# A two-layer transformer block on one core: the retention's key decay, its output scale, transposes in the first stage, earlier modulations and weights kept for the last block

## The chip, the cores and the metric

The kernel runs on one core of a Trainium2 chip. A core has TensorE (matmuls, PE in the rows; PEld is its weight load), VectorE (DVE), ScalarE (ACT), GpSimd (POOL) and SyncE (SP, which issues most DMAs). Each engine works through its own instructions in order and waits on semaphores for the others. Matmul operands lie in SBUF, results in PSUM, eight banks of 128 partitions by 512 floats. The metric is the device time of one execution in microseconds; the median of several runs is given.

## The reference

Two layers (`DEPTH` = 2) of a block on 512 tokens x and 256 context tokens z, 1024 wide:

```python
def hybrid_layer(x, z, c, c_ctx, p, rope_ret, rope_mla, need_ctx):
    mod_x = jax.nn.silu(c) @ p['w_ada'] + p['b_ada']
    mod_z = jax.nn.silu(c_ctx) @ p['w_ada'] + p['b_ada']
    ...
    hx = x * (1.0 + sc1x) + sh1x
    hz = z * (1.0 + sc1z) + sh1z
    mix_x, mix_z = token_mixers(hx, hz, p, rope_ret, rope_mla, need_ctx)
    x = layer_norm(DEEPNORM_ALPHA * x + g1x * mix_x, ...)
    x = layer_norm(DEEPNORM_ALPHA * x + g2x * sq_relu_mlp(x * (1.0 + sc2x) + sh2x, p), ...)
    (z likewise where need_ctx, that is in the first layer alone)
```

`token_mixers` sums three gated branches: retention (four heads in chunks, forward and backward, keys multiplied by a decay that depends on the position, a norm per head and a gain `ret_gn_gain`), neighbourhood attention (eight heads) and latent attention (eight heads), and multiplies the sum with `w_out`. `sq_relu_mlp` is relu squared between two weights of 1024 by 4096 and back. Six vectors of modulation per layer and token kind (shift, scale, gate, twice) come from `w_ada`.

## The kernel before

**Arithmetic.** Everything is held feature-major, 128 features in the partitions. A product in float32 accuracy is three fast matmuls: each operand is split into a high part (ScalarE, `hi_of`, line 388) and what is left (VectorE, `lo_of`, line 391), and `mm3` (lines 438 to 440) adds high by high, high by low, low by high. A weight unit is 128 by 1024 floats, 512 KB: `load` fetches it into one of three `wraw` buffers, `weight` splits it into one of three `wsp` pairs, or, with `own=True`, into two tiles of the large pool.

**Memory.** Large tiles (`dbl`, 4 KB per partition) come from a pool of 30, small ones (`sgl`, 2 KB) from one of 13. PSUM has banks of tags `pd` (three: projections and most else), `pst` (two: transposes, retention outputs), `pso` (one) and `pss` (scores).

**Order.** The Python code traces instructions; a scheduler then sets each engine's order by its own estimate of when an instruction is ready. `tc.keep_in_program_order` pins an instruction behind the one traced before it on its engine. What runs beside what is written by hand: `Fill` holds jobs (projections, gates, the retention's preparation) that are fed between the steps of a `pipeline` by their TensorE cost, and `Paced` advances a generator by a rate (`step`) or up to a count (`until`).

**Stages, in order of time.** The *opening* (lines 1592 to 1656, to about 70 us) computes conditioning, modulates the input and multiplies with the first four weights, in a loop over eight slices k of 128 features. For slice k the scale's modulation is a TensorE product (`modulation_pe`, line 495, into a `pso` bank, read at line 497); the shift's is one on VectorE (`modulation`, line 515, one product for x and one for z); `affine_split` (lines 600 to 602) forms the operands; `outer` multiplies them. Then latent attention (`mla`, to about 500 us; 40 items of three steps in the first layer, with a function `tick` called after each), neighbourhood attention (`Natten`), and retention in two runs, `ret.run(0)` and `ret.run(1)`, each prepared by `prep` as a fill job. In `prep` the rotated keys are transposed on TensorE into `pd` banks (line 1285), multiplied by the decay (line 1291, tile `ktf`), and split, tile by tile (lines 1292 and 1293). An item of the retention has scores (688, 1368), outputs (1392 to 1396), the norm (1402 to 1412) and a transposition (1419) whose result is multiplied by the gain and a half (line 1424).

The remaining modulations of the first layer (gate, shift, scale, gate: units 16 to 47) and all 48 of the second are computed on VectorE by `modulations`, one unit after another: while the gates' fill jobs run (`ADA_GATES` = 0.3 of a unit per us of fill), in the last branch (`ADA_BRANCH`), in the output product (`ADA_OUT`) and in the MLP (`ADA_MLP`). The first 24 (`ROOMY`) fetch their weights into large tiles two ahead, the rest through the single `graw` buffer. Then follow the three branches (lines 1467 to 1513), the output product with the first norm, the MLP in eight blocks j, of `ff1` (four units) and `ff2` (four units), and the second norm. In the second layer (`need` false) the first and the last block of the MLP run in two rounds of 256 tokens each, and each round loads and splits its weights anew (line 1815).

Of the kernel before, what the change touches and what calls it, by code (L numbers as in the profile page):

```python
# [10 lines left out]
BF16 = mybir.dt.bfloat16  # L11
# [6 lines left out]
D = 1024  # L18
# [17 lines left out]

WIDE = 64
# [10 lines left out]

ROOMY = 24
# [3 lines left out]
ADA_BRANCH = 0.05  # L53
# [264 lines left out]
def block_kernel(ctx, tc, xT, zT, cond, wu, sp, bias, tab, out):  # L318
# [148 lines left out]

    silu = [dram.tile([1, D], F32, name=f"silu{i}") for i in range(2)]
# [23 lines left out]
    def modulation_pe(ps, l, c, raw, v):  # L492

        for k in range(KT):
            pe.matmul(ps, raw[:, 128 * k : 128 * k + 128], v[:, :, k].unsqueeze(2).broadcast_to([128, 2, WIDE // 2]), start=k == 0, stop=k == KT - 1)
        m = mods[l][:, c, :]
        dve.tensor_scalar(m, ps[:, :, 0], 0.5, spt[l][:, SP_BADA + c : SP_BADA + c + 1], op0=ALU.mult, op1=ALU.add)
        adjust(m, c)
# [46 lines left out]
    def modulations(units, cs, roomy):  # L545

        def fetch(i):
            if i < len(units):
                t = dbl("ada") if i < roomy else graw.tile([128, 1024], F32, tag="graw", name=nm("graw"))
                sync.dma_start(t, wu[IDX[units[i][0], "ada", units[i][1]]])  # L550
                raws.append(t)

        units, raws = list(units), []
        fetch(0)
        if roomy:
            fetch(1)
        yield
        for i, u in enumerate(units):
            modulation(*u, raws[i], cs, True)
            if len(raws) < i + 2 or i + 2 < roomy:  # L560
                fetch(len(raws))
            yield
# [212 lines left out]
    def mla(l, hx, hz, need, qn, kn, kr, res, want, ahead):  # L775
# [194 lines left out]
        def tick(t):  # L970

            if t == len(items) // 2 - 4:
                fetch_values(1)
            if t == len(items) // 2 + 1:
                for _ in prep_values(1):
                    pass

# [190 lines left out]
    class Retention:  # L1168
# [39 lines left out]
        def prep(self, p2):  # L1208
# [71 lines left out]
            kt = new_tiles(512, 6)  # L1280
            for src, i0 in ((k32, 0), (kz32, 4)):
                nt = src.shape[-1] // 128
                ps = bank_d()
                for i in range(nt):
                    pe.transpose(ps[:, 128 * i : 128 * i + 128], src[:, 128 * i : 128 * i + 128], ident)
                for i in range(nt):
                    t = kt[i0 + i]
                    v = ps[:, 128 * i : 128 * i + 128].rearrange("p (h d) -> p h d", h=2).unsqueeze(2).broadcast_to([128, 2, 2, 64])
                    dk = self.kd[:, i % 2, 2 * p2 : 2 * p2 + 2, :].unsqueeze(3).broadcast_to([128, 2, 2, 64])
                    f = sgl("ktf")[:, :256]  # L1290
                    dve.tensor_tensor(f.rearrange("p (h t d) -> p h t d", h=2, t=2), v, dk, op=ALU.mult)  # L1291
                    hi_of(t[:, :256], f)
                    lo_of(t[:, 256:], f, t[:, :256])
# [53 lines left out]
        def item(self, p2, o, c):  # L1347
# [66 lines left out]
            def s2():  # L1414
# [9 lines left out]
                dve.tensor_scalar(dst, ps, spt[self.l][:, SP_GN + h : SP_GN + h + 1], 0.5, op0=ALU.mult, op1=ALU.mult)  # L1424
# [167 lines left out]
    def opening():  # L1592
# [17 lines left out]
        def inputs(k):  # L1610

            for kind in (1, 0):
                raw = dbl("ada")
                fetch_in(raw, wu[IDX[0, "ada", 8 * kind + k]])
                if kind:
                    modulation_pe(bank_o()[:, :WIDE].rearrange("p (t r) -> p t r", t=2), 0, 8 * kind + k, raw, v)
# [45 lines left out]
    for l in range(DEPTH):  # L1662
# [27 lines left out]
        mla(l, hx, hz, need, qn, kn, kr, y_mla, want[0], na.start)  # L1690
# [6 lines left out]
        if l == 0:  # L1697
            later = Paced(modulations([(0, c) for c in range(16, 48)] + [(1, c) for c in range(48)], conditioning_again(), ROOMY))
# [26 lines left out]
        for c in branch(l, 0, sizes, ops[2], g_mix, total, yop):  # L1725
            later.step(c * ADA_BRANCH)
# [20 lines left out]
        later.until(1 + 8)  # L1747
        for r, (b, cols) in enumerate(rounds):
# [25 lines left out]
            later.until(1 + 24)  # L1774
# [3 lines left out]
        acc = [new_tiles(n, KT) for _, n in bufs]  # L1778
        if need:
            hx, hz = None, None  # L1780
            h_next = [None, None]
        for j in range(8):
            apart = j in (0, 7)
            for rnd in [[r] for r in rounds] if apart else [[(b, slice(0, n)) for b, (_, n) in enumerate(bufs)]]:
# [29 lines left out]
                for i in range(4):  # L1814
                    w = weight(l, "ff2", j, i)
# [90 lines left out]
```

## Time and profile before

| | |
|---|---|
| median of 3 runs | 2592.39 us (2590.51 to 2593.95) |
| the profiled execution | 2591.01 us |
| its span, first to last instruction | 2589.2 us |
| TensorE busy | 2508.3 us (97%) |
| VectorE busy | 1749.9 us (68%) |
| ScalarE busy | 1170.0 us (45%) |
| GpSimd busy | 134.1 us (5%) |
| mean granted TensorE clock | 0.990 of full |

Matmuls are pipelined, so a busy TensorE is not one at its peak. In a line of a timeline stand the start in us, the time taken, engine, line of the kernel, operation, tiles (out<-in), shape and count, and in brackets the idle time of that engine just before and what ended it. A table of stretches gives for each its length and, by engine, the busy time in it with the number of instructions in brackets, then the granted clock (PEclk), the share of the DMA engines that were busy and GB/s.

### The profile page before, as it was taken

The page shows a single profiled execution, that of the slowest core. Times are in us where ns is not written, and L with a number is a line of the kernel's source. Part 1 is how long each engine was busy: PE and PEld are TensorE (multiplying, and loading weights), DVE is VectorE, ACT ScalarE, POOL GpSimd, SP SyncE. Part 2 cuts the span into 40 slices and gives each one's busy share as a digit, 9 for nine tenths or more (in the row PEclk, how much of TensorE's full clock was granted, in tenths as well). Part 3 has the DMA queues.
Part 4 walks back from the last instruction along what each step waited for, and adds up shares of the span by engine and source line. Part 5 has one row for each costly group of instructions (what it writes and reads, how often), then busy time and mean ns, then how long its engine had stood idle before and what let it go on. Part 6 is the DMA issues. An engine that isn't in the chain of part 4 may idle for free.

```text
span 2589.2 us, 40118 instructions
## 1 busy us (share of the span) xinstructions
PE 2508.3 (97%) x15354; PEld 2236.2 (86%) x15354; DVE 1749.9 (68%) x3432; ACT 1170.0 (45%) x2224; POOL 134.1 (5%) x121
## 2 busy tenths in 40 slices
PE   8999999999999999999999999999999899999997
PEld 7999998988888887888888888889898788988887
DVE  6566556788968885676556767665668768744457
ACT  2555545565334345222222446554556544732325
POOL 0100000111000000000000000010011000000000
PEclk8999999999999999999999999999999999999999
DMA  6322224534855533444344424323554466433333
GB/s 244 95 70 90 70 89 125 157 100 128 289 180 176 186 113 106 130 131 134 128 138 131 136 82 140 94 84 102 151 157 119 134 192 195 146 99 98 98 98 123
DMA packets 151317, 340.47 MB, mean 131 GB/s; under 512 B 18642, under 2 KB 58962, under 8 KB 151124
## 3 DMA queue, kind: packets, MB, share of 16 engines
q1 hardware_dynamic: 140756, 322.17, 40.4%
q10 hardware_dynamic: 10368, 15.73, 1.6%
q8 instruction: 121, 1.98, 0.3%
q14 instruction: 72, 0.59, 0.1%
HBM read 288.27 MB, written 36.45 MB: 125 GB/s over the span
## 4 chain that ended last, share of the span: by engine, by line
PE 80%; DVE 9%; ACT 4%; issue 4%; DMA 2%; POOL 1%; SPq 1%; POOLq 0%; ACTq 0%; DVEq 0%
PE pd L440 19%; PE pd L438 19%; PE pd L439 19%; PE pd L660 3%; PE pd L662 3%; PE pso L629 3%; PE pd L661 3%; PE pst L612 3%; DVE wsp L391 1%; PE pss L688 1%; PE pss L439 1%; PE pss L438 1%; PE pss L440 1%; PE pst L1392 1%; ACT wsp L388 1%
## 5 line engine op out<-in xcount | busy, mean ns | idle before, releaser
L438 PE MATMUL pd<-op,wsp 128*128 128x512 f32 (+1 forms) x3080 | 1069.1, 348 | 19.1 <-ACT wsp L388 5.0
L440 PE MATMUL pd<-op,wsp 128*128 128x512 f32 (+1 forms) x3080 | 1062.3, 346 | 13.7 <-DVE wsp L391 13.2
L439 PE MATMUL pd<-op,wsp 128*128 128x512 f32 (+1 forms) x3080 | 1066.5, 346 | 3.3 <-DVE op L391 1.6
L438 PEld LDWEIGHTS pd<-op,wsp 128*128 128x128 f32 x3080 | 586.0, 191 | 92.2 <-ACT wsp L388 7.0
L440 PEld LDWEIGHTS pd<-op,wsp 128*128 128x128 f32 x3080 | 585.1, 190 | 85.8 <-DVE wsp L391 15.2
L439 PEld LDWEIGHTS pd<-op,wsp 128*128 128x128 f32 x3080 | 586.7, 191 | 70.6 <-DVE op L391 3.3
L388 ACT ACTIVATE wsp<-wraw 128x1024 fp32r<-128x1024 f32 x317 | 334.1, 1055 | 390.2 <-PE pd L440 269.1
L391 DVE TENSOR_TENSOR wsp<-wraw,wsp 128x1024 fp32r<-128x1024 f32 x317 | 386.2, 1221 | 170.4 <-ACT wsp L388 169.5
L660 PE MATMUL pd<-wsp,op 128*128 128x256 f32 x704 | 202.7, 288 | 7.4 <-DVE ktf L1291 3.7
L662 PE MATMUL pd<-wsp,op 128*128 128x256 f32 x704 | 200.7, 285 | 0.5 <-DVE wsp L391 0.5
L661 PE MATMUL pd<-wsp,op 128*128 128x256 f32 x704 | 200.5, 285 | 0.0
L1793 DVE TENSOR_TENSOR rl<-rl 128x256 f32<-128x256 f32 (+1 forms) x104 | 58.9, 567 | 152.2 <-ACT rl L1792 152.1
L1792 ACT ACTIVATE rl<-pd 128x256 f32<-128x256 f32 (+1 forms) x104 | 51.9, 499 | 231.2 <-PE pd L440 230.9
L391 DVE TENSOR_TENSOR pt<-pst,pt 128x512 fp32r<-128x512 f32 (+1 forms) x208 | 121.6, 603 | 42.9 <-ACT pt L388 41.0
L660 PEld LDWEIGHTS pd<-wsp,op 128*128 128x128 f32 x704 | 136.3, 194 | 9.4 <-DVE ktf L1291 4.1
L1807 DVE TENSOR_TENSOR t<-pd,t 128x512 f32<-128x512 f32 (+1 forms) x132 | 80.9, 616 | 89.4 <-PE pd L440 89.0
L662 PEld LDWEIGHTS pd<-wsp,op 128*128 128x128 f32 x704 | 136.2, 193 | 0.7 <-DVE wsp L391 0.7
L661 PEld LDWEIGHTS pd<-wsp,op 128*128 128x128 f32 x704 | 136.3, 194 | 0.0
L388 ACT ACTIVATE pt<-pst 128x512 fp32r<-128x512 f32 (+1 forms) x208 | 105.2, 529 | 52.6 <-PE pst L612 38.3
L629 PE MATMUL pso<-pt,t 128*128 128x256 f32 x704 | 114.5, 292 | 5.1 <-DVE tx L636 2.2
L515 DVE CUSTOM_DVE_ANT_0 cond<-graw,cond,sp 128x1024 bf16<-128x1024 f32 x80 | 102.4, 1280 | 17.3 <-DMA graw<-wu 17.1
L1451 ACT ACTIVATE gate<-pd 128x512 f32<-128x512 f32 x72 | 37.8, 525 | 157.6 <-PE pd L440 153.3
(280 smaller groups left out, 3444.0 us busy)
## 6 DMA issues: line engine op xcount, KB each, us to landing
wraw<-wu SPq DMA_DIRECT2D x327, 512.0 KB, 3.7
graw<-wu SPq DMA_DIRECT2D x56, 512.0 KB, 3.6
ada<-wu SPq DMA_DIRECT2D x40, 512.0 KB, 5.6
gg<-gate ACTq DMA_DIRECT2D x48, 256.0 KB, 2.0
gl<-gg SPq DMA_DIRECT2D x48, 256.0 KB, 3.3
zbias<-bias SPq DMA_DIRECT2D x64, 128.0 KB, 2.3
t<-vd SPq DMA_DIRECT2D x28, 256.0 KB, 5.6
gd<-gt SPq DMA_DIRECT2D x40, 128.0 KB, 2.3
```

The costliest lines, as they stand in the source:

```text
L388: act.activation(R(dst), src, AF.Copy, scale=scale)
L391: (eng or dve).tensor_tensor(R(dst), src, hi, op=ALU.subtract)
L438: pe.matmul(ps, R(a[0]), R(b[0]), start=start, stop=False)
L439: pe.matmul(ps, R(a[0]), R(b[1]), start=False, stop=False)
L440: pe.matmul(ps, R(a[1]), R(b[0]), start=False, stop=stop)
L515: i = dve.tensor_tensor_reduce(cs[2], raw, cs[t], 0.5, spt[l][:, SP_BADA + c : SP_BADA + c + 1], ALU.mult, ALU.add, mods[l][:, c, t : t + 1])
L612: pe.transpose(ps[:, 128 * k : 128 * k + 128], src[:, 128 * (a + k) : 128 * (a + k) + 128], ident)
L629: pe.matmul(o, R(vts[k]), R(pts[k]), start=k == 0, stop=k == n - 1)
L660: pe.matmul(ps, R(a[0]), R(w[0][:, o : o + 256]), start=k == 0, stop=False)
L661: pe.matmul(ps, R(a[1]), R(w[0][:, o : o + 256]), start=False, stop=False)
L662: pe.matmul(ps, R(a[0]), R(w[1][:, o : o + 256]), start=False, stop=k == nk - 1)
L1807: dve.tensor_tensor(a, ps, a, op=ALU.add)
```

## The change

In `prep` all decay multiplications of a bank are issued first, into small tiles that hold two of them, and the split then takes two key tiles at a time. The scale of the retention's output moves from VectorE to ScalarE; the half is put into the gain at the start. In the opening, twelve transposes of the identity are put behind the TensorE modulation of slice 1 and six behind that of slice 2, into the same PSUM tile, ahead of the read at line 497. Units 16 to 23 of the first layer's modulations are computed in the second half of the latent attention, with large tiles of their own; the rest follow where they did, with 16 in place of 24 fetched far ahead, and none in the last branch. In the second layer's last MLP block, the `ff2` weights split in the first round are kept in large tiles for the second.

```diff
+N_STIR = {1: 12, 2: 6}
...
+ADA_EARLY = range(16, 24)
...
-ADA_BRANCH = 0.05
...
+        b = t[:, SP_GN : SP_GN + 4]
+        dve.tensor_scalar(b, b, 0.0, 0.5, op0=ALU.add, op1=ALU.mult)
...
+    def stir(ps, n):
+
+        for _ in range(n):
+            tc.keep_in_program_order(pe.transpose(ps[:, 128:256], ident, ident))
+
+    def modulation_pe(ps, l, c, raw, v, then):
 
         for k in range(KT):
             pe.matmul(ps, raw[:, 128 * k : 128 * k + 128], v[:, :, k].unsqueeze(2).broadcast_to([128, 2, WIDE // 2]), start=k == 0, stop=k == KT - 1)
+        then()
         m = mods[l][:, c, :]
...
+    def modulations_early(units):
+
+        cs = [dbl("silu") for _ in range(2)] + [dbl("prod").bitcast(BF16)[:, :D]]
+        for t in range(2):
+            sync.dma_start(cs[t], silu[t].partition_broadcast(128))
+        raws = []
+
+        def fetch(i):
+            t = dbl("ada")
+            sync.dma_start(t, wu[IDX[units[i][0], "ada", units[i][1]]])
+            raws.append(t)
+
+        fetch(0)
+        yield
+        for i, u in enumerate(units):
+            if i + 1 < len(units):
+                fetch(i + 1)
+            modulation(*u, raws[i], cs, True)
+            yield
...
+            if beside and t > len(items) // 2 + 2 and t % 2:
+                beside.advance()
+
...
-            kt = new_tiles(512, 6)
+            ktt = [dbl("kt") for _ in range(3)]
+            kt = [h for t in ktt for h in halves(t, 512)]
...
+                fs = [sgl("ktf") for _ in range(nt // 2)]
                 for i in range(nt):
-                    t = kt[i0 + i]
...
-                    f = sgl("ktf")[:, :256]
+                    f = fs[i // 2][:, 256 * (i % 2) : 256 * (i % 2) + 256]
                     dve.tensor_tensor(f.rearrange("p (h t d) -> p h t d", h=2, t=2), v, dk, op=ALU.mult)
-                    hi_of(t[:, :256], f)
-                    lo_of(t[:, 256:], f, t[:, :256])
+
+                for i in range(0, nt, 2):
+                    t = ktt[(i0 + i) // 2].rearrange("p (i e n) -> p e i n", i=2, e=2)
+                    f = fs[i // 2].rearrange("p (i n) -> p i n", i=2)
+                    hi_of(t[:, 0], f)
+                    lo_of(t[:, 1], f, t[:, 0])
...
-                dve.tensor_scalar(dst, ps, spt[self.l][:, SP_GN + h : SP_GN + h + 1], 0.5, op0=ALU.mult, op1=ALU.mult)
+                act.activation(dst, ps, AF.Copy, scale=spt[self.l][:, SP_GN + h : SP_GN + h + 1])
...
+                    modulation_pe(ps[:, :WIDE].rearrange("p (t r) -> p t r", t=2), 0, 8 * kind + k, raw, v, lambda: stir(ps, N_STIR.get(k, 0)))
...
+        beside = Paced(modulations_early([(0, c) for c in ADA_EARLY])) if l == 0 else None
+        mla(l, hx, hz, need, qn, kn, kr, y_mla, want[0], na.start, beside)
+        if beside:
+            beside.rest()
...
+            later = Paced(modulations([(0, c) for c in range(16, 48) if c not in ADA_EARLY] + [(1, c) for c in range(48)], conditioning_again(), ROOMY - len(ADA_EARLY)))
...
         for c in branch(l, 0, sizes, ops[2], g_mix, total, yop):
-            later.step(c * ADA_BRANCH)
+            pass
...
-        later.until(1 + 8)
+        later.until(1 + 8 - len(ADA_EARLY))
...
+        last_ff2 = {}
+
+        def ff2_weight(j, i):
+
+            if need or j < 7:
+                return weight(l, "ff2", j, i)
+            if i in last_ff2:
+                return last_ff2.pop(i)
+            last_ff2[i] = weight(l, "ff2", j, i, own=True)
+            return last_ff2[i]
+
...
-                    w = weight(l, "ff2", j, i)
+                    w = ff2_weight(j, i)
```

## Rows read from the trace of the kernel before

**Rows 1.** Stretches of 50 us, busy time by engine, granted clock, DMA share, GB/s.

```profile
500.00:550.00 50.00, 49.04 (x341) 44.49 (x341) 36.74 (x84) 32.72 (x75) 9.47 (x9) 1.00 0.48 140
...
2000.00:2050.00 50.00, 39.62 (x243) 35.09 (x242) 43.62 (x118) 31.28 (x70) 5.78 (x6) 0.91 0.39 110
```

**Rows 2.** Stretches of 2 us, the same columns.

```profile
26.00:28.00 2.00, 2.00 (x13) 1.91 (x13) 0.46 (x2) 0.31 (x1) 0.00 (x0) 0.69 1.02 402
...
40.00:42.00 2.00, 2.00 (x9) 1.62 (x9) 1.65 (x5) 0.60 (x1) 0.00 (x0) 0.90 0.78 168
...
638.00:640.00 2.00, 2.00 (x11) 2.00 (x10) 1.98 (x6) 1.48 (x5) 0.00 (x0) 0.50 0.10 28
...
862.00:864.00 2.00, 1.79 (x8) 1.49 (x9) 2.00 (x5) 0.77 (x2) 0.00 (x0) 1.00 0.41 104
```

**Rows 3.** Timeline of TensorE in the opening, times in us.

```profile
25.25 0.73 PE L438 MATMUL pd<-op,wsp 128*128 128x512 f32 x2 [2.36 <-ACT op L601]
...
26.28 3.06 PE L495 MATMUL pso<-v_cond,ada 128*128 128x64 f32 x16
...
31.46 0.80 PE L439 MATMUL pd<-op,wsp 128*128 128x512 f32 x1 [1.37 <-DVE op L602]
...
42.25 1.89 PE L495 MATMUL pso<-v_cond,ada 128*128 128x64 f32 x16
...
47.52 1.89 PE L495 MATMUL pso<-v_cond,ada 128*128 128x64 f32 x16
```

**Rows 4.** Timeline of TensorE near 477 us.

```profile
476.67 0.28 PE L662 MATMUL pd<-wsp,op 128*128 128x256 f32 x1
...
476.79 0.60 PE L612 MATMUL pst<-ctab,p 128*128 128x128 f32 x4
```

**Rows 5.** Timeline of ScalarE at 477 us.

```profile
477.05 0.38 ACT L388 ACTIVATE nv<-pd 128x256 fp32r<-128x256 f32 x1 [0.36 <-PE pd L662]
```

**Rows 6.** Timeline of VectorE in the opening.

```profile
22.93 0.22 DVE L497 TENSOR_SCALAR mod<-pso,sp 128x2 f32<-128x2 f32 x1 [2.32 <-PE pso L495]
```

**Rows 7.** Groups by line and form: count, busy us, mean ns, idle before.

```profile
L1424 DVE TENSOR_SCALAR ry<-pso,sp 128x256 f32<-128x256 f32 x20 | 9.3, 467 | 0.1
...
L1395 ACT ACTIVATE ro<-pst 128x256 f32<-128x256 f32 x40 | 13.6, 376 | 10.9 <-PE pst L1392 9.7 <-DVE pf L391 0.9 <-ACT wsp L388 0.3
...
L601 ACT ACTIVATE op<-z,mod 128x256 fp32r<-128x256 f32 x8 | 4.8, 599 | 6.1 <-DVE mod L515 6.1
...
L515 DVE CUSTOM_DVE_ANT_0 cond<-graw,cond,sp 128x1024 bf16<-128x1024 f32 x80 | 102.4, 1280 | 17.3 <-DMA graw<-wu 17.1
```

**Rows 8.** Timeline of TensorE in the last branch.

```profile
862.21 0.50 PE L438 MATMUL pd<-op,wsp 128*128 128x512 f32 x1 [1.44 <-DVE ms L1509]
```

**Rows 9.** Timeline of TensorE in the retention.

```profile
637.36 0.38 PE L660 MATMUL pd<-wsp,op 128*128 128x256 f32 x1 [3.06 <-DVE ktf L1291]
```

**Rows 10.** Timeline of VectorE in the retention.

```profile
633.95 0.39 DVE L1291 TENSOR_TENSOR ktf<-pd,kd 128x256 f32<-128x256 f32 x1
...
636.89 1.07 DVE L1291 TENSOR_TENSOR ktf<-pd,kd 128x256 f32<-128x256 f32 x3
```

**Rows 11.** Three longer stretches, all engines.

```profile
671.00:741.00 70.00, 70.00 (x405) 61.87 (x404) 65.27 (x110) 20.74 (x35) 0.53 (x1) 1.00 0.85 298
...
300.00:480.00 180.00, 179.01 (x1213) 162.76 (x1211) 113.53 (x239) 96.67 (x215) 16.78 (x16) 1.00 0.35 104
...
2562.00:2576.00 14.00, 10.73 (x79) 9.57 (x77) 13.19 (x30) 6.24 (x14) 0.00 (x0) 1.00 0.17 58
```

**Rows 12.** The same view, line 515's instructions alone.

```profile
671.00:741.00 70.00, 51.55 (x80) 1.00 0.85 298
```

**Rows 13.** Timeline of VectorE in the last branch.

```profile
859.59 1.28 DVE L515 CUSTOM_DVE_ANT_0 cond<-ada,cond,sp 128x1024 bf16<-128x1024 f32 x1
```

**Rows 14.** Timeline of TensorE at the end.

```profile
2564.70 0.38 PE L440 MATMUL pd<-op,wsp 128*128 128x256 f32 x1 [0.63 <-DVE wsp L391]
...
2570.26 0.39 PE L440 MATMUL pd<-op,wsp 128*128 128x256 f32 x1 [1.57 <-DVE wsp L391]
```

More of the change, by code (lines that the diff above doesn't have):

```diff
@@ L490, in conditioning @@
         return v, cs
-    def modulation_pe(ps, l, c, raw, v):
+    def stir(ps, n):
+        for _ in range(n):
+            tc.keep_in_program_order(pe.transpose(ps[:, 128:256], ident, ident))
+    def modulation_pe(ps, l, c, raw, v, then):
         for k in range(KT):
             pe.matmul(ps, raw[:, 128 * k : 128 * k + 128], v[:, :, k].unsqueeze(2).broadcast_to([128, 2, WIDE // 2]), start=k == 0, stop=k == KT - 1)
+        then()
         m = mods[l][:, c, :]
@@ L772, in result, with mla @@
             return o
-    def mla(l, hx, hz, need, qn, kn, kr, res, want, ahead):
+    def mla(l, hx, hz, need, qn, kn, kr, res, want, ahead, beside=None):
         qtab, ktab = sgl("qtab"), sgl("ktab")
@@ L1615, in inputs @@
                 if kind:
-                    modulation_pe(bank_o()[:, :WIDE].rearrange("p (t r) -> p t r", t=2), 0, 8 * kind + k, raw, v)
+                    ps = bank_o()
+                    modulation_pe(ps[:, :WIDE].rearrange("p (t r) -> p t r", t=2), 0, 8 * kind + k, raw, v, lambda: stir(ps, N_STIR.get(k, 0)))
                 else:
@@ L1689, in block_kernel @@
         score_banks(1)
-        mla(l, hx, hz, need, qn, kn, kr, y_mla, want[0], na.start)
+        beside = Paced(modulations_early([(0, c) for c in ADA_EARLY])) if l == 0 else None
+        mla(l, hx, hz, need, qn, kn, kr, y_mla, want[0], na.start, beside)
+        if beside:
+            beside.rest()
         score_banks(2)
@@ L1697, in block_kernel @@
         if l == 0:
-            later = Paced(modulations([(0, c) for c in range(16, 48)] + [(1, c) for c in range(48)], conditioning_again(), ROOMY))
+            later = Paced(modulations([(0, c) for c in range(16, 48) if c not in ADA_EARLY] + [(1, c) for c in range(48)], conditioning_again(), ROOMY - len(ADA_EARLY)))
         ret.run(0, want[2])
@@ L1773, in block_kernel @@
                 pend.step()
-            later.until(1 + 24)
+            later.until(1 + 24 - len(ADA_EARLY))
             pend.add(layer_norm(l, 0, tok, uu, st, [cut(p, cols) for p in h2[b]], l, 3, nothing))
         acc = [new_tiles(n, KT) for _, n in bufs]
+        last_ff2 = {}
[6 more added lines that the diff above has]
+            return last_ff2[i]
         if need:
```

## The prediction

> **What bounds the kernel now.** I read the profile page first: TensorE is busy nearly all of the time, so a change pays only where TensorE stands idle or runs at its lower clock. Next came the table of 50 us stretches, for where that is: the opening, the retention and the transitions around it lose most, while in attention and in the MLP TensorE is all but full. In [rows 1] compare 500 to 550 us (1.0 us lost, VectorE at 36.7 of 50) and 2000 to 2050 us (10.4 us lost, VectorE at 43.6). The granted clock by 2 us [rows 2] shows stretches at half clock (0.50, that is 1.2 instead of 2.4 GHz) behind such holes. Last, the timelines of single engines say what each hole waited for.
>
> The profiled execution took 2591.0 us, 1.8 us more than its span of 2589.2; the median of the runs is 2592.4, 1.4 above it. The sum below is one of differences, so I take it off the median. A difference under 0.2% (5.2 us) can't be told from none.
>
> **The transposes in the first stage.** The loop over eight rows of the input has TensorE work of 5.27 us a step when it is full (42.25 to 47.52) [rows 3]. Before that it stood idle 2.36 us (until 25.25) and 1.37 us (until 31.46), and in the stretch 26 to 28 the clock fell and came back only in 40 to 42 [rows 2]. From the modulation of step 2 (26.28) to that of step 4 (42.25) it took 15.97 us; two full steps are 10.54. So 5.4 us is all that a warm clock can give, and 4.0 if the 1.37 us hole stays. The cost: a transpose of this form is about 0.11 us behind another (four in 0.60, one being 0.28) [rows 4], so twelve are 1.3 us and six 0.65. They write the same PSUM bank that line 497 reads. That such a read waits for all writes to its bank before it, rows show: line 388 reads the first half of a bank at 477.05, released by the matmuls into the second half (the last began at 476.67), not by its own [rows 4, 5]. So line 497, at 22.93 now [rows 6], comes 1.3 us later, and behind it in VectorE's order stands the shift's product of 1.28 us [rows 7], whose result the operand needs. If that order stays, the idle time is only moved, and the change costs 1.3 us at full clock, 1.3 more for the six at half clock: +2.6 at worst. If VectorE takes the products first (it idled 2.32 us ahead of line 497 [rows 6], and the order is made anew when the kernel is built), line 497 follows the transposes directly, TensorE resumes when it does now, and 1.3 of the 2.36 us idle is filled. A hole of 1.44 us elsewhere [rows 8] had no fall of the clock behind it [rows 2]. I take -4.0, range -5.4 to +2.6.
>
> **The keys' decay in one go.** In the second preparation of layer 0 TensorE stood 3.06 us until 637.36, waiting for line 1291 [rows 9]. That line reads the transposed keys out of two of the three banks of tag pd. VectorE began it at 633.95 and came to the last three only at 636.89 [rows 10], with the splits and the retention's small operations between. Four in a row, at 0.34 us from one to the next, would be through at 635.3, some 2.0 us earlier. Behind the hole the clock is at 0.50 [rows 2], a loss of about 1.7 us over 3.4 us. If the hole shrinks to 1.1 us, shorter than the one of 1.44 us that left the clock alone, that goes too: -3.7. If the first of the four comes later, nothing goes. The other three preparations show 0.6 us of such waits together. The splits become three of 512 columns each on ScalarE and VectorE in place of six of 256, at 0.6 to 0.7 us in place of 0.4, which frees about 0.5 us of both per preparation. I take -3.0, range -4.3 to 0.
>
> **ScalarE scales the outputs.** 20 operations of 467 ns leave VectorE (9.3 us), and 20 come to ScalarE, at 376 ns by its copy of the same form from PSUM up to 599 ns by one with two per-partition operands [rows 7]: 7.5 to 12 us. VectorE is the fuller in the retention (43.6 against 31.3 of 50) [rows 1]. Gaps directly behind line 1424 are short, though, and three retention gaps wait for ScalarE. I take -1.0, range -3 to +1.5. The Trainium skill, in "ScalarE: Activation LUTs", section "Rules for kernel authors", would have it the other way, multiplications on VectorE; by that rule this part is worth 0 and the forecast 1.0 higher. The halving of the gain, two small operations added at the start, lies in VectorE's idle time before 7 us, while TensorE runs its first matmuls: nothing.
>
> **Early modulations.** Eight units of the first layer, two products of 1280 ns each plus an adjustment of about 0.17, move to the second half of the latent attention: 21.9 us of VectorE, one unit every second item. 300 to 480 us has TensorE at 179.0 of 180 and VectorE at 113.5; 671 to 741 us has 20 such units (40 products, each with a short read of its sum), VectorE at 65.3 of 70, and TensorE lost nothing [rows 11, 12]. That is one end, 0. The other is attention at the VectorE load that this reaches, 500 to 550 us: 1.0 us in 50, so 3.5 in 180 where 1.0 is lost now, +2.5. I take +1.5, since attention's softmax stands closer on VectorE than the gates' weight splits. The DMAs (the two broadcast loads and eight of 512 KB, on SP's queue ahead of weight loads) meet engines at 0.35 of their time [rows 11]: nothing. The product leaves the branch stage: there two units lay, one of them just ahead of line 1509 [rows 13] in VectorE's queue, for which TensorE then waited 1.44 us [rows 8]: -1.5, range -2.6 to 0. In the gates' stage only 16 instead of 24 weights are now fetched far ahead; by 741 us the last four units go through one buffer, whose load starts only when the unit before is done, with weight splits and gated sums queued on VectorE behind the wait. In the MLP that buffer cost VectorE 17.1 us in 80 products [rows 7], TensorE nothing: +0.5, range 0 to +3. Together +0.5. The slots: three of the 30 large tiles are held through half the attention and two more in turn; no row shows a wait for a slot, and its price is left to the slower rival.
>
> **Kept last blocks.** In the second round of the last MLP block, four weights are no longer loaded and split. From 2562 to 2576 us TensorE is busy 10.73 of 14 us and VectorE 13.19 [rows 11]: VectorE is the bound. Two holes there wait for line 391's splits, 0.63 and 1.57 us [rows 14]. Those two are the least, 2.2; all 3.27 us of idle TensorE is the most, since three splits of 1.22 us (3.7 us) stand in that stretch. Eight large tiles hold the kept weights; by my count of the code 28 of 30 are then in use. I take -2.8, range -3.3 to 0 (if a slot is missing). The norm behind it stays.
>
> **Sum.** -4.0 - 3.0 - 1.0 + 0.5 - 2.8 = -10.3: 2582.1 us.
>
> **The rivals.** (1) The opening's clock falls all the same, and the twelve lie on the path: +1.3 in place of -4.0, 2587.4. For it: VectorE's present order, and that no row shows transposes alone at either level. The Trainium skill, "TensorE: Matmul & The Clock Gate", section "Part 4: PE-mode transpose", says that transposes do not count as busy for the clock as matmuls do; if that holds here, this rival is the outcome. (2) Besides that, the retention's gaps move on: the engines work in order, its next step (line 1392 or 1419) waits for ScalarE or for the group norm, and parts two and three are worth 0: 2591.4. Against it: the hole at 637 is a wait for a bank, which is freed early whatever comes next. (3) Slower: the early products stand in VectorE's queue ahead of a row maximum or a reciprocal, and TensorE has nothing else in order. If all eight units did so, it would be 21.9 in place of 1.5, 2602.5; from half of them on (11 us) the change is a loss. Against it: other projections are interleaved there, and 671 to 741 us bore 20 units for nothing.
>
> **How the numbers follow.** Forecast 0.48 (own range 2576 to 2587), rival one 0.24, two 0.14, three 0.14. Faster by over 0.2% means under 2587.2: 0.45 of the forecast, half of rival one (0.12), 0.02 of two, together 0.59. Slower, over 2597.6: 0.12 of rival three and 0.01 of two, 0.13. The rest, 0.28, is within. The range reaches from 2573 (all parts at their best ends, 18.6 us off, give 2573.8) to 2595, past rival two; it leaves out most of rival three and a little below.
>
> **What would show it.** Right: no stretch at 0.50 between 26 and 40 us and line 495's fifth group near 37 instead of 42.25; the wait for line 1291 under 1.5 us and no half clock behind it; no hole for line 391 in the last 15 us; TensorE at 178 or more of 180 from 300 to 480 us. Wrong: a second idle time behind the transposes as long as now, new waits for ScalarE's copies ahead of line 1419, VectorE's products ahead of TensorE's holes in attention, or another order of the instructions in stages that the change doesn't touch, each worth a microsecond or two.

## The result and the profile after

| | before | after |
|---|---|---|
| median of 6 runs | 2593.22 us (2590.51 to 2596.58) | 2579.65 us (2576.98 to 2582.50) |
| ratio of after to before, 95% interval | | 0.9942 (0.9931 to 0.9954) |
| the profiled execution, its span | 2591.0, 2589.2 us | 2580.2, 2578.4 us |
| TensorE, VectorE, ScalarE busy | 2508.3, 1749.9, 1170.0 us | 2506.2, 1738.0, 1176.2 us |

The change is faster by 0.58%; on the median given with the kernel before (2592.39 us) that is 15.0 us (11.9 to 17.9). The two medians differ by 13.6 us. The forecast was 10.3, at 2582.1 us. TensorE's work is the same but for eighteen transposes; what went is idle time (80.9 to 72.2 us in the two profiles) and half clock (53.7 to 47.9 us).

To see where, take the same instruction in both traces and subtract. Timeline of TensorE after, times in us:

```profile
26.22 0.74 PE L441 MATMUL pd<-op,wsp 128*128 128x512 f32 x2 [1.16 <-ACT op L633]
...
37.78 1.89 PE L506 MATMUL pso<-v_cond,ada 128*128 128x64 f32 x16
...
81.99 0.47 PE L441 MATMUL pd<-op,wsp 128*128 128x512 f32 x1 [1.37 <-DVE pr L802]
...
561.57 0.63 PE L644 MATMUL pst<-ctab,p 128*128 128x128 f32 x4 [1.13 <-DVE p L655]
...
619.13 0.39 PE L692 MATMUL pd<-wsp,op 128*128 128x256 f32 x1 [0.88 <-ACT rz L1279]
...
630.87 0.35 PE L692 MATMUL pd<-wsp,op 128*128 128x256 f32 x1 [1.90 <-DVE ktf L1327]
...
646.17 0.62 PE L1459 MATMUL pso<-ctab,ro 128*128 128x128 f32 x2 [2.21 <-DVE pf L394]
...
649.29 0.59 PE L441 MATMUL pd<-op,wsp 128*128 128x512 f32 x1
...
853.66 0.40 PE L441 MATMUL pd<-op,wsp 128*128 128x512 f32 x1
...
1487.83 0.50 PE L443 MATMUL pd<-op,wsp 128*128 128x512 f32 x1 [2.20 <-DVE wsp L394]
...
2222.07 0.39 PE L443 MATMUL pd<-op,wsp 128*128 128x256 f32 x1 [1.58 <-DVE wsp L394]
...
2565.35 0.63 PE L769 MATMUL pso<-ones,lns 128*128 128x64 f32 x4 [1.13 <-DVE lns L1570]
```

The same places in the kernel before, as far as [rows 3, 8, 9] don't show them:

```profile
87.14 0.47 PE L438 MATMUL pd<-op,wsp 128*128 128x512 f32 x1 [1.37 <-DVE pr L770]
...
566.31 0.63 PE L612 MATMUL pst<-ctab,p 128*128 128x128 f32 x4 [1.12 <-DVE p L623]
567.55 0.38 PE L660 MATMUL pd<-wsp,op 128*128 128x256 f32 x1 [0.61 <-DVE ktf L1291]
...
624.38 0.39 PE L660 MATMUL pd<-wsp,op 128*128 128x256 f32 x1 [0.85 <-ACT rz L1244]
...
652.71 1.70 PE L1392 MATMUL pst<-t,pf 128*128 128x256 f32 x12 [1.89 <-DVE ro L1396]
654.43 0.47 PE L438 MATMUL pd<-op,wsp 128*128 128x512 f32 x1
...
1496.12 0.50 PE L440 MATMUL pd<-op,wsp 128*128 128x512 f32 x1 [2.20 <-DVE wsp L391]
...
2230.61 0.39 PE L440 MATMUL pd<-op,wsp 128*128 128x256 f32 x1 [1.58 <-DVE wsp L391]
...
2576.77 0.63 PE L737 MATMUL pso<-ones,lns 128*128 128x64 f32 x4 [1.21 <-DVE lns L1530]
```

| place, us before | after minus before | what lies between |
|---|---|---|
| fifth modulation of the opening, 42.25 | -4.47 | the transposes |
| start of attention, 87.14 | -5.15 | the rest of the opening |
| neighbourhood attention, 566.31 | -4.74 | the early modulations: +0.41 |
| retention, 624.38 | -5.25 | a hole of 0.61 for line 1291 gone |
| behind the hole for line 1291, 637.36 | -6.49 | that hole 1.90 in place of 3.06 |
| behind the next hole, 654.43 | -5.14 | given back |
| in the last branch, 862.21 | -8.55 | the two products gone from it |
| in the MLP, 1496.12 | -8.29 | the output product |
| second layer's MLP, 2230.61 | -8.54 | its retention, nothing |
| last norm, 2576.77 | -11.42 | the kept weights: -2.88 |
| end of the span, 2589.2 | -10.8 | the last norm, at half clock in both (10.4 us of it, 9.3 before) |

So the opening gave somewhat more than forecast, the end came as forecast, the branch gave more, and the keys' part, the second largest term, gave nothing in the end. One pair of executions carries chance of 2 us and more, though, as the experiments show; the parts are therefore weighed by the ratios of many runs.

### The profile page after: what moved, and what is told of

It reads as the page before. It is cut to its first block, busy times and chain, and to the rows that moved or that the text cites. A ratio compares the mean times of both kernels' runs of the same rounds, so it can differ in the third digit from the quotient of the medians.

```text
span 2578.4 us, 40118 instructions
## 1 busy us (share of the span) xinstructions
PE 2506.2 (97%) x15372; PEld 2234.8 (87%) x15372; DVE 1738.0 (67%) x3398; ACT 1176.2 (46%) x2228; POOL 137.3 (5%) x121
## 4 chain that ended last, share of the span: by engine, by line
PE 77%; DVE 11%; ACT 5%; issue 3%; DMA 2%; POOL 1%; SPq 0%; POOLq 0%; ACTq 0%; DVEq 0%
PE pd L443 19%; PE pd L442 19%; PE pd L441 19%; PE pd L694 3%; PE pd L692 3%; PE pd L693 3%; PE pso L661 3%; PE pst L644 3%; DVE wsp L394 2%; PE pss L441 1%; PE pss L442 1%; PE pss L443 1%; ACT wsp L391 1%; DMA wraw<-wu 1%; ACT ro L1450 1%
## 5 line engine op out<-in xcount | busy, mean ns | idle before, releaser
L441 PE MATMUL pd<-op,wsp 128*128 128x512 f32 (+1 forms) x3016 | 1050.7, 349 | 14.5 <-ACT wsp L391 3.7
L443 PE MATMUL pd<-op,wsp 128*128 128x512 f32 (+1 forms) x3016 | 1044.7, 347 | 11.0 <-DVE wsp L394 10.5
L442 PE MATMUL pd<-op,wsp 128*128 128x512 f32 (+1 forms) x3016 | 1048.3, 348 | 1.9 <-DVE op L394 1.4
L441 PEld LDWEIGHTS pd<-op,wsp 128*128 128x128 f32 x3016 | 573.8, 191 | 85.9 <-ACT wsp L391 5.5
L443 PEld LDWEIGHTS pd<-op,wsp 128*128 128x128 f32 x3016 | 573.3, 190 | 83.3 <-DVE wsp L394 12.9
L442 PEld LDWEIGHTS pd<-op,wsp 128*128 128x128 f32 x3016 | 574.7, 191 | 69.4 <-DVE op L394 2.6
L391 ACT ACTIVATE wsp<-wraw 128x1024 fp32r<-128x1024 f32 x309 | 326.2, 1058 | 384.3 <-PE pd L443 261.8
L394 DVE TENSOR_TENSOR wsp<-wraw,wsp 128x1024 fp32r<-128x1024 f32 x309 | 377.2, 1223 | 167.3 <-ACT wsp L391 166.3
```

Source lines behind the costliest of these rows:

```text
L391: act.activation(R(dst), src, AF.Copy, scale=scale)
L394: (eng or dve).tensor_tensor(R(dst), src, hi, op=ALU.subtract)
L441: pe.matmul(ps, R(a[0]), R(b[0]), start=start, stop=False)
L442: pe.matmul(ps, R(a[0]), R(b[1]), start=False, stop=False)
L443: pe.matmul(ps, R(a[1]), R(b[0]), start=False, stop=stop)
```

## The experiments

### Each part alone

Five kernels have one part of the change each. A part's diff is that of the part in the text above, so only its core stands here.

**The keys' decay in one go.**

```diff
+                fs = [sgl("ktf") for _ in range(nt // 2)]
...
-                    hi_of(t[:, :256], f)
-                    lo_of(t[:, 256:], f, t[:, :256])
...
+                for i in range(0, nt, 2):
...
+                    hi_of(t[:, 0], f)
+                    lo_of(t[:, 1], f, t[:, 0])
```

> The kernel before with the keys' decay in one go and nothing else. In the trace of the whole change TensorE gained 2.75 us on the kernel before at the hole that stood at 637 us, and lost 2.7 us again over the next 15 us, where a hole of 2.21 us now brings the clock to half. Theory one (the giving back belongs to this part: TensorE comes earlier to the same chain of the norm, which is no earlier): the same picture here, gain of 2.7 and loss of 2.7, and the run within 0 to -1.0 us of the kernel before. Theory two (the giving back came from ScalarE's scaling, which put copies ahead of the norm's operations): the gain stays here, -3 to -4 us, and no half clock behind the hole at 652.

Measured: ratio 1.0002 (0.9994 to 1.0011), median 2592.8 us. Theory one. Timeline of TensorE in this kernel, the two holes:

```profile
637.17 0.36 PE L660 MATMUL pd<-wsp,op 128*128 128x256 f32 x1 [2.27 <-DVE ktf L1292]
...
652.14 2.73 PE L1397 MATMUL pst<-t,pf 128*128 128x256 f32 x12 [2.60 <-DVE ro L1401]
```

The first hole is 0.8 us shorter than before (3.06), the second 0.7 longer (1.89). The half clock has moved behind the second: its twelve matmuls take 2.73 us, where they took 1.70.

**ScalarE scales the outputs.**

```diff
-                dve.tensor_scalar(dst, ps, ..., 0.5, op0=ALU.mult, op1=ALU.mult)
+                act.activation(dst, ps, AF.Copy, scale=spt[self.l][:, SP_GN + h : SP_GN + h + 1])
```

> The kernel before with only the output scale moved from VectorE to ScalarE. Theory one (it takes nothing from the path and adds nothing): within 1 us of the kernel before, the retention's holes of 3.06 and 1.89 us as they were. Theory two (ScalarE's copies delay the norm): +1 to +3 us in the retention. My forecast had -1.0 (-3 to +1.5).

Measured: 0.9990 (0.9981 to 0.9999), -2.6 us (-4.9 to -0.3), median 2590.5. By the middle neither theory's number: it gives a little. The interval reaches to -0.3, into theory one's 1 us. Its group by line and form, then its two holes in the retention:

```profile
L1427 ACT ACTIVATE ry<-pso,sp 128x256 f32<-128x256 f32 x20 | 9.4, 469 | 5.7 <-PE pso L1422 5.6
```

```profile
638.37 0.58 PE L663 MATMUL pd<-wsp,op 128*128 128x256 f32 x1 [2.69 <-DVE ktf L1294]
...
652.78 0.44 PE L1422 MATMUL pso<-ctab,ro 128*128 128x128 f32 x2 [1.09 <-DVE pf L391]
```

469 ns on ScalarE in place of 467 on VectorE [rows 7]: what moved is 9.4 us of load, from the fuller engine to the emptier. The holes did not stay as they were, as theory one had it: they are 2.69 and 1.09 us in place of 3.06 and 1.89, 1.2 us less in this one place.

**The transposes.**

```diff
+            tc.keep_in_program_order(pe.transpose(ps[:, 128:256], ident, ident))
```

> The kernel before with only the twelve and six transposes in the opening. Theory one (the transposes keep the clock up by themselves): -5.2 us, all of it before 50 us, no stretch at 0.50 there, and every later stage shifted by the same amount. Rival (part of the opening's gain came from an order of the engines that the other parts brought): the clock falls again near 27 us, and the run is between 0 and +2 us.

Measured: 0.9990 (0.9981 to 0.9999), median 2590.65 us, runs from 2586.1 to 2594.6. In the profile theory one holds: the start of attention is at 82.01 us (87.14 before), no half clock before 600 us. But of these 5.1 us the runs show only 2.6 (0.3 to 4.9), and the profiled execution itself ends 0.3 us ahead of the one before (spans of 2588.9 and 2589.2). It lost the rest at later holes, 2.3 us of it behind 2227 us, where it has 6.8 us at half clock and the kernel before has none. The changed kernel's profile has no such loss: in the table above its lead never falls under 4.7 us.

**The kept last blocks.**

```diff
+            last_ff2[i] = weight(l, "ff2", j, i, own=True)
```

> The kernel before with only the four kept weights of the second layer's last MLP block. Theory one: TensorE gains 2.9 us in the last 45 us of the span, the run -2.3 to -2.9 us, and no hole above 0.6 us that waits for the low part of a split there. Rival (the gain at the end needs the other parts' order): under 1 us.

Measured: 0.9984 (0.9975 to 0.9992), -4.1 us (-6.5 to -2.1), median 2589.1. Theory one; the last norm's matmuls are at 2573.79 us, 2.98 ahead of before, and at 2530 us, ahead of the block, this profile was 0.1 late. This kernel shows something else as well: up to the last block it has the same instructions in the same order as the kernel before, yet its trace wanders against it. TensorE's timeline and two stretches of it:

```profile
88.11 0.47 PE L438 MATMUL pd<-op,wsp 128*128 128x512 f32 x1 [1.37 <-DVE pr L770]
...
864.14 0.50 PE L438 MATMUL pd<-op,wsp 128*128 128x512 f32 x1 [1.17 <-DVE ms L1509]
```

```profile
656.00:658.00 2.00, 2.00 (x6) 1.57 (x5) 1.14 (x5) 0.87 (x3) 0.90 (x1) 0.50 0.19 66
888.00:890.00 2.00, 1.55 (x11) 1.35 (x12) 2.00 (x3) 0.82 (x1) 0.00 (x0) 1.00 0.20 18
```

Against before it is 0.97 us late at 88 us (half clock in the opening for longer) and 1.93 at 864 [rows 8]. It is at half clock at 656, where before was at 1.00, and at full clock at 888, where before was at 0.50. So which of such holes takes the clock down differs from one execution to the next.

**The early modulations, with the empty branch.**

```diff
+            if beside and t > len(items) // 2 + 2 and t % 2:
+                beside.advance()
...
-            later.step(c * ADA_BRANCH)
+            pass
```

> The kernel before with only the early modulations, and with them the empty last branch and the 16 weights fetched far ahead. In the trace of the whole change TensorE lost 0.4 us in the second half of the latent attention and gained 3.2 us in the last branch (848 to 863 us), of which the forecast had +1.5 and -1.5. Theory one (both are this part's own): -2.5 to -4 us against the kernel before, the holes of 0.6 and 1.44 us for line 1509's sums gone or halved. Theory two (the branch gained because other parts had moved it against the weight loads): +0.5 us, as forecast, with the hole of 1.4 us still there.

Measured: 0.9994 (0.9985 to 1.0002), -1.6 us (-3.9 to +0.5), median 2593.2 beside 2594.4 of the kernel before in these runs. Theory one in kind. The hole of 1.44 us is gone; those of 0.58 and 0.60 are there still:

```profile
852.87 0.39 PE L439 MATMUL pd<-op,wsp 128*128 128x256 f32 x1 [0.55 <-DVE ms L1533]
855.16 0.47 PE L439 MATMUL pd<-op,wsp 128*128 128x512 f32 x1 [0.60 <-DVE ms L1533]
```

**The branch emptied, and nothing moved ahead.** Of the change only this:

```diff
-            later.step(c * ADA_BRANCH)
+            pass
```

> The kernel before without the two modulation units in the last branch (they follow in the output product, before their due time), nothing else changed. Theory one (the two products in VectorE's queue cost the branch 2 to 3 us, and eight early units are not needed for it): -1.5 to -3 us if the output product bears them, the same holes gone as with the early modulations. Theory two (the two units only go from one place with a hole to another): 0 within 1 us, a new hole between 900 and 945 us.

Measured: 1.0000 (0.9992 to 1.0009). Theory two: the hole of 1.44 us goes from the branch, and another stands in the output product, which has to take the units over (20 of line 515's instructions from 896 to 946 us, 16 before). TensorE's timeline:

```profile
921.86 0.65 PE L743 MATMUL pss<-ctab,tiny 128*128 128x128 f32 x4 [1.49 <-POOL tiny L1543]
```

The early units are what lets the branch go empty without a bill behind it: the kernel with them has no such hole there.

The five parts alone sum to 0.5 - 2.6 - 2.6 - 1.6 - 4.1 = -10.4 us; the whole is 15.0 (11.9 to 17.9). With 2.2 us of interval on each part the sum is known to about 5, so that parts help each other is not shown.

### The change without one part

**Without the transposes**, against the changed kernel:

```diff
-                    modulation_pe(..., 0, 8 * kind + k, raw, v, lambda: stir(ps, N_STIR.get(k, 0)))
+                    modulation_pe(..., 0, 8 * kind + k, raw, v)
```

> The whole change without its transposes. Alone they gave 2.2 us in the median, though TensorE was 5.0 us earlier at 60 us in the profile. Theory one (the gain in the opening is whole, and what came back later was chance of that kernel's clock): the run is 5 us slower than the changed kernel, 8 us faster than the kernel before. Theory two (about half of what the opening gains is lost behind it, at holes where the clock falls more often when the opening doesn't hold it): 2 to 3 us slower than the changed kernel, 10 to 11 us faster than the kernel before.

Measured: 0.9965 (0.9952 to 0.9978), 9.1 us faster than the kernel before, 6.0 slower than the whole change. That fits theory one (5 us) better than theory two (2 to 3), and the run of the transposes alone (2.6) fits theory two. The intervals overlap; between 2.6 and 6.0 the worth of the transposes stays open.

**Without the keys' part**, against the changed kernel:

```diff
-                for i in range(0, nt, 2):
...
-                    hi_of(t[:, 0], f)
...
+                    hi_of(t[:, :256], f)
+                    lo_of(t[:, 256:], f, t[:, :256])
```

> The whole change without its first part: the keys' decay tile by tile as before. Alone that part gave nothing (ratio 1.0002, interval 0.9994 to 1.0011), where the forecast had 3.0 us; in the trace of the whole change the 2.75 us gained by 644 us were lost again by 660 us. Theory one (the gain is given back by the hole behind it, in company too): within 1.5 us of the changed kernel (2579.7), the hole of 3 us near 632 us with half clock behind it, and a hole near 647 us that leaves the clock alone. Theory two (in company of the other parts it pays): 3 us or more slower than the changed kernel.

Measured: 0.9945 (0.9933 to 0.9958), median 2579.7 us, the same as the whole change. Theory one. TensorE's two holes in this kernel, and then, in the first layer's output product, one that comes up again below:

```profile
633.00 0.38 PE L692 MATMUL pd<-wsp,op 128*128 128x256 f32 x1 [2.69 <-DVE ktf L1326]
...
647.57 0.44 PE L1454 MATMUL pso<-ctab,ro 128*128 128x128 f32 x2 [1.10 <-DVE pf L394]
...
925.25 0.50 PE L443 MATMUL pd<-op,wsp 128*128 128x512 f32 x1 [2.20 <-DVE wsp L394]
```

2.69 and 1.10 us without the part, 1.90 and 2.21 with it: 3.8 and 4.1 together. The half clock lies behind the first hole here, and behind the second in the changed kernel. A stretch of the changed kernel:

```profile
646.00:648.00 2.00, 1.83 (x8) 1.67 (x9) 2.00 (x11) 0.66 (x3) 0.00 (x0) 0.57 0.70 273
```

What is late at the second hole is a chain that the part doesn't touch. VectorE and then ScalarE in the changed kernel:

```profile
642.27 0.16 DVE L1447 SCALAR_TENSOR_TENSOR sh<-mv,rs 128x4 f32<-128x4 f32 x1 [0.71 <-POOL rs L1445]
...
643.08 1.22 DVE L394 TENSOR_TENSOR wsp<-wraw,wsp 128x1024 fp32r<-128x1024 f32 x1
644.21 0.69 DVE L1451 TENSOR_TENSOR ro<-ro,gt 128x512 f32<-128x512 f32 x1
```

```profile
642.47 1.66 ACT L1450 ACTIVATE ro<-ro,sh,rs 128x128 f32<-128x128 f32 x4 [1.37 <-DVE sh L1447]
```

GpSimd's power, VectorE's shift, 1.66 us of scaling on ScalarE, a product by the gate on VectorE (behind a weight's split, 643.08) and a sum, done at 645.70: the norm of one item. TensorE's transposition (646.17) is released, by the profile, by a split of the scores that is queued on VectorE right behind that sum. TensorE, through the first hole earlier, reaches this chain earlier and waits for it.

### What transposes do to the clock

**Sixty in place of twelve**, in the kernel with the transposes alone:

```diff
-N_STIR = {1: 12, 2: 6}
+N_STIR = {1: 60, 2: 6}
```

> The kernel before with sixty transposes in place of twelve behind slice 1's modulation, some 7 us in which TensorE does nothing else. If transposes keep the clock as matmuls do, the granted clock stays at 1.00 through them and behind them, and the time is that of the kernel with twelve plus 4.5 us (48 of 0.12 us, less the 1.16 us hole). If they don't, the clock is at 0.50 within or behind the sixty, the transposes there take twice as long, and the time is 3 to 7 us more than that.

TensorE's timeline, then stretches of 2 us:

```profile
22.42 6.72 PE L497 MATMUL pso<-ctab 128*128 128x128 f32 x60
```

```profile
26.00:28.00 2.00, 2.00 (x21) 2.00 (x20) 0.00 (x0) 0.00 (x0) 0.00 (x0) 1.00 1.03 404
28.00:30.00 2.00, 1.69 (x16) 1.45 (x14) 0.78 (x3) 0.56 (x1) 0.00 (x0) 1.00 1.06 404
```

For 6.7 us TensorE does nothing else, 0.11 us each, and the clock stays at 1.00 through them and behind them. The time is 2595.2 us, in one run, the span 4.4 longer than with twelve (2593.3 and 2588.9), where 4.5 was expected; but only 2.7 of it stand at the start of attention, so that the sum fits is luck. The clock doesn't depend on one execution: in all seven profiles of kernels without these transposes it is at half in the opening, for 13.7 or 17.1 us, and in none of the six with both groups. Such transposes keep the clock up here as matmuls do.

**The twelve without the six**, in the changed kernel:

```diff
-N_STIR = {1: 12, 2: 6}
+N_STIR = {1: 12}
```

> The changed kernel with the twelve transposes behind slice 1's modulation and without the six behind slice 2's. Theory one (the clock falls for the first hole, and the six are not needed): no half clock before 50 us, a hole of about 1.4 us at 29 us back, 0 to 1.4 us slower than the changed kernel. Theory two (the second hole takes the clock down by itself): half clock from about 30 us on, 4 to 6 us slower than the changed kernel, as without any.

Measured: 0.9952 (0.9939 to 0.9966), median 2581.6 us, runs from 2575.4 to 2586.4. TensorE's second hole in the opening, and a stretch behind:

```profile
30.77 0.50 PE L442 MATMUL pd<-op,wsp 128*128 128x512 f32 x1 [1.48 <-DVE op L634]
```

```profile
34.00:36.00 2.00, 2.00 (x11) 2.00 (x11) 0.00 (x0) 0.00 (x0) 0.00 (x0) 0.50 1.02 387
```

In the profiled execution theory two: behind the second hole the clock is at half from 31 to 38 us, and TensorE is 3.5 us later at the start of attention than in the changed kernel. But this execution is the slowest of the five. Two of them had a mean granted clock of 0.988 (2584.1 and 2586.4 us), three of 0.990 to 0.992 (2575.4 to 2581.6), so the clock may fall at this hole in some executions only. By the ratios leaving out the six costs 2.6 us (0.9952 and 0.9942, overlapping), between the theories: that the six are needed is likely and not shown.

### More transposes, in other holes

The remedy of the opening was tried at five other holes with half clock behind them; `warm(n)` is `stir` with a bank of its own, called in `mm3` ahead of the third product and ahead of an item's transposition:

```diff
+        if between:
+            warm(between)
...
+                if (self.l, p2, o, c) in WARM:
+                    warm(WARM[self.l, p2, o, c])
```

> The changed kernel with more transposes of the identity, each group in a hole behind which its trace shows half clock: 16 in the first layer's output product (the hole of 2.20 us at 925), 9 and 20 in the first MLP block (1.45 and 2.88 us at 962 and 965), 24 in the second layer's retention (3.54 us at 1999), 16 in a gate's product there (2.17 us at 2034): 85 of 0.11 to 0.12 us, 10 us of transposes in 12 us of holes. Theory one (the half clock behind a hole costs TensorE its full price, as in the opening): the 27 us at 0.50 between 926 and 2043 us shrink to under 10, and the run is 5 to 9 us faster than the changed kernel. Theory two (the matmuls behind those holes wait for VectorE at either clock, so a faster TensorE only waits longer): the half clock goes, and the run is within 2 us. Theory three (the transposes push the waiting products back): slower by up to 5 us.

Measured: 0.9952 (0.9938 to 0.9965), median 2580.8 us: no faster than the changed kernel. Of the 30.6 us at half clock between 926 and 2043 us 13.6 are left in its profile; what one place gains the others lose, between theories two and three. TensorE's timeline:

```profile
924.77 1.91 PE L510 MATMUL pso<-ctab 128*128 128x128 f32 x16
...
2003.40 0.39 PE L701 MATMUL pd<-wsp,op 128*128 128x256 f32 x1 [2.42 <-ACT ra L1277]
...
2012.67 2.78 PE L510 MATMUL pso<-ctab 128*128 128x128 f32 x24
...
2039.18 1.97 PE L510 MATMUL pso<-ctab 128*128 128x128 f32 x16 [1.59 <-ACT ry L1475]
```

In the output product the half clock goes, and the products behind are 2.8 us earlier against the changed kernel than ahead of it. In the first MLP block the nine and the twenty shorten holes of 1.45 and 2.88 us to 0.54 and 0.69, and the products behind come 0.1 us earlier: TensorE waits longer at the next weight. In the retention the order of the stage, made anew, has a hole of 2.42 us for ScalarE at 2003 and the twenty-four only at 2013, where they fill nothing and take 2.8 us; at 2039 us the sixteen themselves waited 1.59 us for their PSUM bank. So the one group that seemed to pay was run alone:

```diff
+                finish(f, fm_groups(w, 0, [(yy, n)], KT, 16 if l == 0 and r == 1 and f == 5 else 0)[0])
```

> The changed kernel with only the first of the added groups: 16 transposes in the first layer's output product, in the hole of 2.20 us at 925. With all five groups TensorE gained 2.8 us there in the profile (no half clock at 926 to 933) and nothing at the other four, where it waits for another engine a little later at either clock; that kernel was level with the changed one. Theory one (this group pays where TensorE is the bound behind the hole, about 20 us of products that wait for nothing): 1.5 to 3 us faster than the changed kernel. Theory two (what is gained there is lost behind it): within 1 us.

Measured: 0.9932 (0.9919 to 0.9946), median 2577.1 us, the fastest of all. Theory one by its size (2.6 us), though the intervals overlap (0.9931 to 0.9954 for the changed kernel), so that it beats the changed kernel is not shown. Nor is it shown that the sixteen keep the clock: in two kernels without them, with the early modulations alone and without the keys' part, the same hole of 2.20 us has no half clock behind it either. And of the 4.5 us by which this profile is shorter than the changed kernel's, only 0.3 stand at 1000 us; most of the rest arises in the second layer, which it doesn't touch.

## Why the prediction was right, step by step

The time lies 2.5 us under the forecast and inside its own range (2576 to 2587). By the ratio the change is worth 15.0 us, 4.7 more than forecast, and 10.3 lies outside the interval. The steps were not all right: errors cancel, and that they do so nearly is luck.

**The transposes: right.** Forecast -4.0, of 5.4 at most; at the start of attention the five profiles with twelve and six are 5.1 to 6.5 us ahead of before, and the ratios give 2.6 alone and 6.0 in company. The step that decided it was VectorE's order, and it went as hoped. VectorE after, where line 509 is the old line 497:

```profile
21.37 1.28 DVE L527 CUSTOM_DVE_ANT_0 cond<-ada,cond,sp 128x1024 bf16<-128x1024 f32 x1
...
25.10 0.22 DVE L509 TENSOR_SCALAR mod<-pso,sp 128x2 f32<-128x2 f32 x1 [2.44 <-PE pso L501]
```

The product now stands ahead of the read, and the read waits for the transposes, not the other way round. TensorE's hole is 1.16 us in place of 2.36, 1.2 us less, where the forecast filled 1.3. TensorE resumes at 26.22, 1.0 us later than before, where the forecast had no delay; 0.9 of that stood already ahead of the transposes. A stretch of 2 us after, for [rows 2]:

```profile
26.00:28.00 2.00, 1.78 (x13) 1.64 (x13) 1.90 (x5) 0.78 (x2) 0.00 (x0) 1.00 1.00 393
```

No stretch before 646 us is at half clock. The rival by which the clock falls all the same is out: sixty transposes held it, and so did the twelve and six in all five profiles. The rule of the Trainium skill that the forecast set against this part ("TensorE: Matmul & The Clock Gate", "Part 4: PE-mode transpose") is not borne out here; 6.7 us of nothing but transposes ran at a granted clock of 1.00.

**The keys' decay: wrong.** Forecast -3.0 (-4.3 to 0); measured +0.5 (-1.6 to +2.9) alone and -0.8 as the difference of two ratios in company. The first half of the step was right in kind: the hole shrank, by 1.2 us of the 2.0 forecast, and the half clock behind it went. It is 1.90 us, though, where the forecast's sign was under 1.5, and part of the 1.2 is ScalarE's scaling (2.69 without the keys' part). The four multiplications don't run in a row. VectorE in the changed kernel:

```profile
630.23 0.16 DVE L1447 SCALAR_TENSOR_TENSOR sh<-mv,rs 128x4 f32<-128x4 f32 x1 [0.79 <-POOL rs L1445]
630.31 0.42 DVE L1327 TENSOR_TENSOR ktf<-pd,kd 128x256 f32<-128x256 f32 x1
```

The fourth, which frees the bank, stands behind the norm's shift, and the shift waits 0.79 us for GpSimd: in order, a tensor's last operation is only as early as what was queued ahead of it. The step that failed altogether is the one behind the hole. The text had it as a wait for a bank "which is freed early whatever comes next", as if a hole shortened there were time gained at the end, and put the second rival, by which the retention's gaps move on, at 0.14. For this part that rival is what happened: the next hole grew by about as much (0.7 us for 0.8 alone, 1.1 for 0.8 in company), and the half clock moved behind it.

**ScalarE's scaling: right in sign, mis-sized.** Forecast -1.0; measured -2.6 (-4.9 to -0.3). At one place of the first layer's retention it takes 1.2 us off the two holes, alone (2.69 and 1.09 us) as in the kernel without the keys' part (2.69 and 1.10); the forecast gave the whole part 1.0. Why the holes shrink is not shown. An operation took 469 ns on ScalarE, inside the 376 to 599 of the bounds. The rule of the Trainium skill that keeps multiplications on VectorE ("ScalarE: Activation LUTs", "Rules for kernel authors") gave 0, just outside the interval: the two take the same time here, and VectorE was the fuller.

**The early modulations: mis-sized, in our favour.** Forecast +0.5 in sum, the end of the measured interval: -1.6 (-3.9 to +0.5). Attention was to cost +1.5 and the gates' stage +0.5. Stretches of the changed kernel, for [rows 11]:

```profile
300.00:480.00 180.00, 178.82 (x1217) 162.82 (x1217) 129.31 (x280) 96.68 (x215) 17.74 (x15) 1.00 0.40 123
661.00:731.00 70.00, 70.00 (x404) 61.81 (x403) 62.18 (x107) 22.80 (x41) 1.93 (x1) 1.00 0.77 267
2551.00:2565.00 14.00, 13.22 (x111) 13.01 (x109) 13.56 (x38) 8.08 (x18) 0.00 (x0) 1.00 0.22 76
```

Attention carries 15.8 us more of VectorE and loses 0.2 of TensorE; the same instructions come 0.4 us later. The bound by its load (500 to 550 us, 1.0 lost in 50) was the wrong row to lean to: VectorE at 129 of 180 has room, and 671 to 741 us, at the other end, was the nearer guide. The gates' stage lost nothing. Between the marks at 654 and 862 us the profile gained 3.4 us, 3.0 of it in the branch, where 1.5 was forecast and 2.6 the most; with the early modulations alone it is 1.7 in the branch. That the slower rival would come from here is out.

**The kept blocks: right.** Forecast -2.8 (-3.3 to 0); -2.9 between the marks in the profile, -4.1 (-6.5 to -2.1) by the ratios. In the stretch that answers to 2562 to 2576 us TensorE is busy 13.22 of 14 where it was 10.73, and the two holes for line 391 are gone.

So the total came out because the parts that were thought to cost or to give little (+0.5, -1.0) gave more, and the one of 3.0 gave none. With the values in company for the transposes and the keys (-6.0 and -0.8) and those alone for the rest, the parts sum to -15.1, the whole; with all alone to -10.4. That the excess over the forecast lies in the transposes fits this and is not shown. The range of 2573 to 2595 held all this; the separate terms were known no better than 2 or 3 us each.

## What to carry to other kernels

When a hole is shortened, follow the waiting engine to its next wait and see which chain ends there; if that chain doesn't depend on what was sped up, the gain stops at it, and the half clock that was to be saved can come back behind the next wait. Filling a hole with transposes paid in the opening, where all profiles without them have half clock behind it. It paid nothing at four other holes, where TensorE waits for another engine a little later or the filler itself waits for a buffer of that stage. Gains of 2 or 3 us in 2600 need many runs: with the same instructions, two profiles differed by 1.9 us at the same place.

## What the runs showed of the hardware

The same hole doesn't always take the clock down. In the first layer's output product TensorE waits 2.20 us for a weight's low part in both the changed kernel and the one without the keys' part (925.25 above). The stretch of 2 us behind it, in the changed kernel:

```profile
926.00:928.00 2.00, 1.00 (x2) 0.83 (x3) 2.00 (x5) 0.00 (x0) 0.00 (x0) 0.55 0.12 10
```

and without the keys' part:

```profile
926.00:928.00 2.00, 2.00 (x10) 1.64 (x10) 2.00 (x5) 1.09 (x2) 0.00 (x0) 1.00 0.73 236
```

Half clock from 926 to 933 us in the one, none in the other. A forecast that gives each hole a fixed price for the clock is therefore one of averages: a hole of 1.44 us that left the clock alone in one profile, as the forecast used it, is weak evidence that a like one will, and one of 1.48 us in the opening (30.77 above) had half clock behind it. What decides, the runs don't show.
